# S5's matrices made in two parts: the GpSimd chain, and TensorE's share some FFN steps later

## The chip, the cores and the metric

The kernel runs on one core of a Trainium2 chip. The metric is the device time of one execution in microseconds; a kernel's time is the median of its runs. A profile of one execution gives, for each engine, every instruction with its start and duration, and what released it.

## The reference

Two layers of a decoder trunk on 256 tokens of 1024 features, in float32. Each layer is

```
x = x + 1/2 FFN_1(norm(x))                 # SwiGLU, 2816 hidden
h = norm(x)
x = x + (sum_b sigmoid(gate_b) * y_b) w_out    # b: mLSTM, S5, GLA, RWKV-7, each on 512 columns of h w_in
x = x + CrossAttention(norm(x), norm(mem))
x = x + 1/2 FFN_2(norm(x))
```

The change concerns the branch S5: 32 groups of 16 channels with 64 complex states each, run as a scan over the tokens.

```
bar  = exp(lam * step)                          # complex, one for each state
bb   = ((bar - 1) / lam) * (b_re + i b_im)      # [group, state, channel]
s_t  = bar * s_(t-1) + bb u_t
y_t  = Re(c s_t) + d u_t
z    = gelu(y);  y_b = (z glu_w1) * sigmoid(z glu_w2)
```

## The kernel before

**FFN.** `ffn` (line 377) opens a layer with 22 up steps, `f` = 0 to 21. A step takes a chunk of weights, two halves of 128 x 1024, each loaded by SP's queue (`chunk`, line 227), copied rounded by ScalarE (`whi`, line 242) and split by VectorE (`wlo`, line 243); then 48 TensorE products of 128 x 128 weights with 256 columns (three for each block: lines 257 to 259) and the activation on VectorE and ScalarE. The 8 down steps, `d` = 0 to 7, have 66 products each, and each ends in `x` plus the result (line 410).

**S5's matrices.** They hang on parameters alone, so they are made during the first FFN. `s5_ahead(at)` is called after each step, with `at` = f in the up steps and 22 + d in the down steps, and `S5_AT` says for each layer after which steps `s5_prep` and the four calls of `s5_mats` (line 1101), one for each feature tile, are traced. A call of `s5_mats` does the following:

- three loads from ScalarE's queue: `s5bc` (C) and the last block of `Bp` (B), lines 1111 and 1113
- on GpSimd a chain of complex products over 128 x 128 elements, B and C times powers of the state's factor: 48 operations (lines 1119 to 1135), then a memset of `In` (line 1144)
- on TensorE 8 transposes of `Bp` into the bank `wps` (line 1151), in two halves that ScalarE copies to `W` (line 1152), and 16 products of 64 columns into the bank `gps` (line 1157), which need the first 36 operations of the chain; the transposes need all 48
- ScalarE copies `gps` to `Gs` (line 1160), VectorE adds the skip term in four operations (line 1162), and six DMAs on ScalarE's queue put pieces of `Gs` into `In` (lines 1167 and 1170)

`s5` (line 1175) runs in the mix and takes `W`, `In` and `Cp` of tile after tile in `s5_tile`.

**The order of the work.** The program is traced as one list, and a planner makes each engine's queue from it with its own costs: among the instructions whose inputs are ready by these costs an engine takes the one traced first. `issue_after` adds an order, `high_priority` moves the weights' split to the front, and SP's queue keeps the traced order. On the chip each engine works its queue off in order and waits on semaphores. Tiles in SBUF get their places from the planner by how long they live; `Bp` has 128 x 1280 elements, `W` 128 x 1024. PSUM tiles of one tag share their banks: `wps` is in that of `br="y"`, `gps` in that of `br="s"`, one bank each.

The mix that follows (`mix`, line 601) norms `x` (its squares are summed on GpSimd, line 293, its low parts made there too, line 338) and takes five chunks of columns before the norm is there; then `rwkv` is traced, and the other branches in turns by the letters of `ORDER`.

Of the kernel before, what the change touches and what calls it, by code (L numbers as in the profile page):

```python
# [14 lines left out]
ALU = mybir.AluOpType  # L15
# [7 lines left out]
# of each layer: columns taken before the norm, when the memory is split, where S5's matrices are made, and the  # L23
# order in which the branches of the mix go ahead
LAZY = 5, 5
MEM_AT = 0, 0
S5_AT = (2, 7, 12, 15, 19), (3, 10, 16, 22, 26)
ORDER = ("SSDSSSDSSSGSDSSGSDSGDGDGDGDGDGDDGDGDGMDGMDGMMDMDMMDMDDDDDD",
         "SSSSSSSSSSSSDSDGDGDGDMGDMGDMGDMGDMGDMGDMGDMGDGDGDDDDDDDDDD")
POS = 0, 1, 3, 2, 4                  # where the steps of a block have their rows  # L30
# [23 lines left out]
class Arena:  # L54
    """Small tiles in rotation, cut from one tile."""
# [19 lines left out]
class K:  # L75
# [20 lines left out]
    def px(self, shape, n="px", br=None):  # L96
        """A PSUM bank of the branch at work."""
        br = br or self.br
        return self.ps.tile(shape, F32, tag="px" + br, name=self.nm(n), bufs=self.PX[br])

    def pd(self, n):
        """A PSUM bank for the large products."""
        return self.ps.tile([P, 2, T], F32, tag=self.pdt[0], name=self.nm(n), bufs=self.pdt[1])
# [13 lines left out]
    # ------------------------------------------------------------ set-up  # L117
# [28 lines left out]
    def consts(self):  # L146
# [9 lines left out]
        # an early use of the scalar engine's tables, so that they are there when the data is  # L156
# [5 lines left out]
        # columns for reductions over partitions  # L162
# [4 lines left out]
        # per-head-of-64 selectors (columns)  # L167
# [8 lines left out]
        # takes the mean over a head off  # L176
# [3 lines left out]
        # reset pattern for scans over chunks of 64  # L180
# [3 lines left out]
        # causal masks of a chunk of 64 of the delta rule: rows s (twice), columns t (twice): [r a] in an even  # L184
        # chunk, [a r] in an odd one, with s <= t for r and s < t for a
# [7 lines left out]
        # level masks for GLA: 1 where s in first and t in second half of the same block of 2m  # L193
        self.lvl = {}
        for mm in (16, 8, 4, 2, 1):
# [5 lines left out]
            # s >= 2mm*n  # L201
            nc.gpsimd.affine_select(out=f, in_=f, pattern=[[-2 * mm, nb], [0, 2 * mm]],
                                    compare_op=ALU.is_ge, fill=0.0, base=0, channel_multiplier=1)
            # s < 2mm*n + mm
# [3 lines left out]
        # rows to be spread over partitions: the parts of eight rows from 0 and from 32, and who takes which  # L208
# [11 lines left out]
    # ------------------------------------------------------------ helpers  # L220
# [6 lines left out]
    def chunk(self, dram):  # L227
        """A chunk of 16 blocks of weights, each half loaded and split on its first use: f(block) -> (hi, lo)."""
# [25 lines left out]
    def mm3(self, ps, w, x, first, last):  # L254
        """ps += w.T x in three passes of split operands."""
        nc = self.nc
        nc.tensor.matmul(ps, w[0], x[0], start=first, stop=False)  # L257
        nc.tensor.matmul(ps, w[0], x[1], start=False, stop=False)  # L258
        nc.tensor.matmul(ps, w[1], x[0], start=False, stop=last)  # L259

    def newton(self, x, n, parts=P):
        """1/sqrt(x) for x [parts, n], x > 0."""
# [12 lines left out]
    def bcast_rows(self, stat, groups, out_ps):  # L275
        """stat [128 tok, groups] for one token tile -> out_ps[m, tok] = stat[tok, m // (128 // groups)]."""
# [6 lines left out]
    def rstd_tok(self, x, last=False):  # L283
        """x [128, 8, 256] -> rsqrt(mean(x^2) + eps) [128 tok, tok tile]."""
# [19 lines left out]
    def rstd_row(self, x):  # L304
        """x [128, 8, 256] -> [128, 256] with rsqrt(mean(x^2) + eps) of each token on all partitions."""
        rs = self.sp.tile([P, T], F32, tag="rs", name=self.nm("rs"), bufs=1)
        self.rows(self.rstd_tok(x), rs)
        return rs
# [7 lines left out]
    def gained(self, x, gname):  # L316
        """x times the gain of its norm, split: hi, lo [128, 8, 256]; the rstd is left to the products' readers."""
# [10 lines left out]
    def norm(self, x, gname, rs=None):  # L328
        """RMS norm, split: returns hi, lo tiles [128, 8, 256]."""
# [11 lines left out]
    def prod(self, blk, ps, hi, lo, interleave=False):  # L341
        """ps[:, s, :] = two blocks of outputs over the 8 tiles of hi + lo."""
# [33 lines left out]
    # ------------------------------------------------------------ FFN  # L376
# [37 lines left out]
    def s5_ahead(self, at):  # L414
        """What S5 makes of its parameters alone, on the way."""
        for i, a in enumerate(S5_AT[self.l]):
            if a == at:
                self.s5_mats(i - 1) if i else self.s5_prep()

    # ------------------------------------------------------------ cross attention  # L420
# [8 lines left out]
    def mem_stats(self):  # L429
        """The rstd of the memory's tokens, as a column and as a row."""  # L430
# [12 lines left out]
    def mem_kv(self):  # L443
        """Keys [d, m] and values [m, d] of the memory."""
# [29 lines left out]
    def xattn(self):  # L474
# [20 lines left out]
        rq = self.tp.tile([P, 4], F32, tag="rq", name=self.nm("rq"))        # rstd / 16, and minus it  # L495
# [15 lines left out]
    def softmax(self, h, qs, rq, kT):  # L511
        """Weights of a head, [t, m]."""
# [20 lines left out]
    def head(self, h, e, v):  # L533
        """The output of a head, split."""
# [17 lines left out]
    def proj_k(self, wname, c, hi, lo, acc):  # L552
        """acc += the product over input tiles 2c, 2c + 1 (hi, lo [128, 2, T]); the last one adds to x."""
# [12 lines left out]
    # ------------------------------------------------------------ mixers  # L566
# [9 lines left out]
    def spill(self, t):  # L576
        """Puts a tile away in DRAM; the returned function brings it back."""
# [10 lines left out]
    def wtiles(self, c):  # L588
# [4 lines left out]
        if c < LAZY[self.l]:                            # not yet normed  # L593
# [44 lines left out]
    def dense(self, branches):  # L638
        """The products that wait for nothing else: the gates, and the memory's keys and values."""
# [23 lines left out]
    # ---- C: gated linear attention  # L663
    def gla(self):
# [21 lines left out]
        # log decays (times 16)  # L686
# [19 lines left out]
        # scores, transposed: the blocks of a token tile with itself and of the first with the second; the keys of  # L706
        # two heads are on top of each other, so the queries go in block-diagonally
        A = self.ot([P, 2, 2, 2, P], n="gA")       # [s, pair, tile, par, t]
        Ao = self.ot([P, 2, 2, P], n="gAo")        # [s, pair, par, t]
# [4 lines left out]
        Q = self.ot([P, 2, 4, 2, 64], n="gQ")      # twice [channel, pair and tile, par, t of a second half]  # L714
# [14 lines left out]
        for lv, m in enumerate((128, 64, 32, 16, 8, 4, 2, 1)):  # L729
# [39 lines left out]
            else:  # L769
                # only the second half of each block of 2m has columns to take  # L770
# [5 lines left out]
        # output, token-major  # L776
# [25 lines left out]
        # gate: o * silu(g), twice the value, without the gain  # L802
# [16 lines left out]
    def split_y(self, y, scale=None):  # L819
# [3 lines left out]
        if len(y.shape) == 4:                                        # step by step of blocks of four  # L823
# [5 lines left out]
        elif scale is not None and not isinstance(scale, float):     # a column for each tile  # L829
# [13 lines left out]
    # ---- A: mLSTM  # L843
    def mlstm(self):
# [14 lines left out]
        uc = th                                                # twice silu  # L859
# [8 lines left out]
        v = self.ot([P, 2, 4, P + 1], n="av")                   # with a column of ones, for the sums of weights  # L868
# [15 lines left out]
        # gates: rows 0..3 of R: M (then em at 64.., g at 32..)  # L884
# [30 lines left out]
        num = self.ot([P, 2, W], n="anum")                      # token-major  # L915
        s = sp.tile([P, 16], F32, tag="ast", name=self.nm("asts"))       # den (tt, h), mean square (tt, h)
# [59 lines left out]
        self.tap(f"ml_{l}", out)              # twice the value, without the gain  # L976
# [3 lines left out]
    # ---- B: S5  # L980
    def exp_acc(self, x, n):
        """exp(x) and exp(x) - 1 for x [128, n]."""
# [22 lines left out]
    def s5_prep(self):  # L1005
# [47 lines left out]
        # bar - 1, coef  # L1053
# [18 lines left out]
        # Four steps at a time: with L the state's factor of a step and s[k] the state's share of the steps before  # L1072
        # the block k, times L,
        #   s[k + 1] = L^4 s[k] + sum_q L^(4 - q) B u[4 k + q]
        #   y[4 k + p] = Re(C L^p s[k]) + sum_(q <= p) Re(C L^(p - q) B) u[4 k + q] + D u[4 k + p]
# [7 lines left out]
        # rotations by the steps of 1, 2, ... 64 blocks  # L1083
# [17 lines left out]
    def s5_mats(self, i):  # L1101
        """The matrices of a feature tile (four pairs of groups): input [(q, c), state], state to output
        [state, (p, c)], within a block [(q, c), (p, c)]."""
# [5 lines left out]
        Bp = self.ot([P, 4, 2, 5, 32], n="s5Bp")                     # B times powers 4, 3, 1, 2, 0  # L1109
# [16 lines left out]
        cv = lambda p: (Cp[:, :, 0, p, :], Cp[:, :, 1, p, :])        # of the real and imaginary part of s  # L1126
# [16 lines left out]
        with self.tc.issue_after(last.ins):  # L1143
            nc.gpsimd.memset(In, 0.0)
        W = self.ot([P, 4, 2, P], n="s5W")
# [7 lines left out]
        # Re(C L^m B): rows of L^2 B (m = 2, 3) and of B (m = 0, 1)  # L1153
# [21 lines left out]
    def s5(self):  # L1175
# [3 lines left out]
        for i in range(2):  # L1179
            ps = self.wtiles(15 + i)  # L1180
            up = self.ot([P, 2, 4, 64], n="bup")                # step by step of the blocks
# [3 lines left out]
        self.ys[1] = y, 0.5                   # twice the value  # L1185
        us = self.ot([P, 4, 4, 64], n="us")                     # [(q, c), tile, pair, block]
# [5 lines left out]
        for i in range(4):  # L1192
            yield from self.s5_tile(i, us[:, i], y)

    def s5_tile(self, i, us, y):
        """One feature tile: four pairs of groups."""
# [11 lines left out]
        # v = conj(E) w  # L1208
# [39 lines left out]
    # ---- D: RWKV-7  # L1248
    def rwkv(self):
# [6 lines left out]
        hv = sp.tile([P, 8], F32, tag="hv", name=self.nm("hv"))         # w0 / 2, a0 / 2  # L1256
        TS(hv[:, 0:4], self.vec("w0", 0, 4), 0.5, None, ALU.mult)
        TS(hv[:, 4:8], self.vec("a0", 0, 4), 0.5, None, ALU.mult)
        ka = sp.tile([P, 8], F32, tag="ka", name=self.nm("ka"))         # k_a / 2, 1 - k_a / 2
# [14 lines left out]
        # decay, in-context rate  # L1274
# [25 lines left out]
        # normalised keys  # L1300
# [431 lines left out]
```

## Time and profile before

| | |
|---|---|
| runs of the kernel | 1878.28, 1883.78 and 1884.1 us; median 1883.78 |
| span of the profiled execution, first to last instruction | 1876.7 us |
| the runs, above that span | 1.6 to 7.4 us, the median 7.1 |
| TensorE busy in the span | 1795.8 us (96%) |
| VectorE, ScalarE, GpSimd busy | 1303.0, 913.3, 494.7 us |
| mean granted TensorE clock | 0.978 of 2.4 GHz |

The profiled execution's own time is not listed apart from its span; what lies around a span is seen from the runs. Engines are called PE (TensorE), PEld (its weight loads), DVE (VectorE), ACT (ScalarE), POOL (GpSimd) and SP. In a group's line `out<-in` gives tiles by the program's names. The granted clock is a share of 2.4 GHz.

### The profile page before, as it was taken

Reading aid. Unit: us, or ns where it says so; the run is one execution under the profiler, and the core shown is the slowest. Engines: PE = TensorE matmul, PEld = TensorE weight load, DVE = VectorE, ACT = ScalarE, POOL = GpSimd, SP = SyncE. Lnnn points to the kernel's source line nnn. Section 1 sums busy time; section 2 is a strip of 40 time slices with the busy share of each in tenths; the row PEclk is TensorE's granted clock in tenths of the full one; section 3 lists DMA queues with packets and bytes.
Section 4 is the critical chain, followed back from the end, with each engine's and each line's share of the span. In section 5 each row is a group of like instructions: output and inputs, shape, how many; then the busy total and the mean of one; then the engine's idle time right before and its main releaser. Section 6 shows DMA issues by size and latency. Waiting matters only on the chain. (4 is left out here: it accounts for less than half of the span.)

```text
span 1876.7 us, 37100 instructions
## 1 busy us (share of the span) xinstructions
PE 1795.8 (96%) x14884; PEld 1758.4 (94%) x14884; DVE 1303.0 (69%) x2197; ACT 913.3 (49%) x1434; POOL 494.7 (26%) x733
## 2 busy tenths in 40 slices
PE   7899999999999999999999889999999999999997
PEld 7788999999999999999999888999999999999997
DVE  8766575987566776766597555779775767766653
ACT  4444355455554454544445334555554554545442
POOL 6688321131111130100153675212121003110001
PEclk9999999989999999999999989999999999999998
DMA  6555555446446754565656545644653576546553
GB/s 193 174 149 157 159 178 177 148 131 200 152 147 199 252 178 133 170 184 185 184 161 207 153 139 159 192 146 132 211 153 119 197 240 225 156 131 186 184 184 102
DMA packets 131852, 320.34 MB, mean 171 GB/s; under 512 B 45792, under 2 KB 50912, under 8 KB 131168
## 3 DMA queue, kind: packets, MB, share of 16 engines
q1 hardware_dynamic: 83664, 290.31, 49.1%
q10 hardware_dynamic: 48016, 27.67, 5.2%
q8 instruction: 116, 1.90, 0.4%
q14 instruction: 56, 0.46, 0.1%
HBM read 300.11 MB, written 16.52 MB: 169 GB/s over the span
## 5 line engine op out<-in xcount | busy, mean ns | idle before, releaser
L243 DVE TENSOR_TENSOR wlo<-wraw,whi 128x1024 fp32r<-128x1024 f32 x524 | 670.8, 1281 | 372.0 <-ACT whi L242 361.1
L242 ACT CAST whi<-wraw 128x1024 fp32r<-128x1024 f32 x524 | 546.7, 1046 | 655.5 <-issue 152.9
L259 PE MATMUL gu<-xhi,wlo 128*128 128x256 f32 x1344 | 383.7, 285 | 2.9 <-DVE wlo L243 2.9
L258 PE MATMUL gu<-xlo,whi 128*128 128x256 f32 x1344 | 385.5, 287 | 0.0
L257 PE MATMUL gu<-xhi,whi 128*128 128x256 f32 x1344 | 384.1, 286 | 0.0
L259 PEld LDWEIGHTS gu<-xhi,wlo 128*128 128x128 f32 x1344 | 261.0, 194 | 3.5 <-DVE wlo L243 3.5
L258 PEld LDWEIGHTS gu<-xlo,whi 128*128 128x128 f32 x1344 | 260.9, 194 | 0.6
L257 PEld LDWEIGHTS gu<-xhi,whi 128*128 128x128 f32 x1344 | 260.3, 194 | 0.5
L293 POOL TENSOR_TENSOR arena<-arena 128x256 f32<-128x256 f32 x69 | 72.2, 1046 | 578.9 <-ACT arena L291 576.3
L259 PE MATMUL dn<-ahi,wlo 128*128 128x256 f32 x704 | 200.9, 286 | 0.0
L258 PE MATMUL dn<-alo,whi 128*128 128x256 f32 x704 | 200.7, 286 | 0.0
L257 PE MATMUL dn<-ahi,whi 128*128 128x256 f32 x704 | 200.3, 285 | 0.0
L257 PE MATMUL gps<-hhi,whi 128*128 128x256 f32 x512 | 151.3, 296 | 3.5 <-ACT gst L1517 2.7
L258 PE MATMUL gps<-hlo,whi 128*128 128x256 f32 x512 | 149.6, 292 | 0.0
L259 PE MATMUL gps<-hhi,wlo 128*128 128x256 f32 x512 | 148.9, 291 | 0.0
L259 PEld LDWEIGHTS dn<-ahi,wlo 128*128 128x128 f32 x704 | 136.3, 194 | 0.2
L258 PEld LDWEIGHTS dn<-alo,whi 128*128 128x128 f32 x704 | 136.3, 194 | 0.2
L257 PEld LDWEIGHTS dn<-ahi,whi 128*128 128x128 f32 x704 | 136.1, 194 | 0.2
L257 PE MATMUL zin<-hhi,whi 128*128 128x256 f32 x384 | 111.3, 290 | 1.1 <-ACT gst L1517 1.1
L259 PE MATMUL zin<-hhi,wlo 128*128 128x256 f32 x384 | 109.9, 286 | 0.0
L258 PE MATMUL zin<-hlo,whi 128*128 128x256 f32 x384 | 109.6, 285 | 0.0
L257 PEld LDWEIGHTS gps<-hhi,whi 128*128 128x128 f32 x512 | 100.6, 197 | 6.7 <-ACT gst L1517 4.2
(528 smaller groups left out, 4381.7 us busy)
## 6 DMA issues: line engine op xcount, KB each, us to landing
wraw<-in_gu_dram SPq DMA_DIRECT2D x176, 512.0 KB, 4.0
wraw<-in_dn_dram SPq DMA_DIRECT2D x88, 512.0 KB, 4.2
wraw<-in_win_dram SPq DMA_DIRECT2D x68, 512.0 KB, 4.2
wraw<-in_gates_dram SPq DMA_DIRECT2D x64, 512.0 KB, 4.1
gd<-gst ACTq DMA_DIRECT2D x32, 256.0 KB, 2.1
wraw<-in_wk_dram SPq DMA_DIRECT2D x16, 512.0 KB, 3.7
wraw<-in_wv_dram SPq DMA_DIRECT2D x16, 512.0 KB, 3.6
gld<-gd SPq DMA_DIRECT2D x32, 256.0 KB, 3.9
```

The lines of the kernel that those rows point to most:

```text
L242: nc.scalar.copy(hi, raw)
L243: nc.vector.tensor_tensor(lo, raw, hi.bitcast(F32), ALU.subtract)
L257: nc.tensor.matmul(ps, w[0], x[0], start=first, stop=False)
L258: nc.tensor.matmul(ps, w[0], x[1], start=False, stop=False)
L259: nc.tensor.matmul(ps, w[1], x[0], start=False, stop=last)
L293: nc.gpsimd.tensor_tensor(acc, acc, sq, ALU.add)
```

## The change

`s5_mats` becomes a generator with a `yield` between GpSimd's chain and TensorE's share. `s5_ahead` runs it up to the `yield` at the old steps (`S5_AT`, unchanged); what follows, TensorE's transposes and products, ScalarE's copies, VectorE's additions and the six DMAs into `In`, is traced at the steps of the new `S5_PE`, by `s5_finish`. Step 30 of layer 0 does not occur in `ffn`; `s5` finishes a tile that is still open before it uses it.

```
+S5_PE = (18, 24, 27, 30), (16, 22, 26, 29)
...
     def s5_ahead(self, at):
         for i, a in enumerate(S5_AT[self.l]):
             if a == at:
-                self.s5_mats(i - 1) if i else self.s5_prep()
+                if i:
+                    self.s5_late[i - 1] = self.s5_mats(i - 1)
+                    next(self.s5_late[i - 1])
+                else:
+                    self.s5_late = {}
+                    self.s5_prep()
+        for i, a in enumerate(S5_PE[self.l]):
+            if a == at:
+                self.s5_finish(i)
+
+    def s5_finish(self, i):
+        if i in self.s5_late:
+            for _ in self.s5_late.pop(i):
+                pass
...
         In = self.ot([P, 4, P], n="s5In")
         with self.tc.issue_after(last.ins):
             nc.gpsimd.memset(In, 0.0)
+        yield
         W = self.ot([P, 4, 2, P], n="s5W")
...
         for i in range(4):
+            self.s5_finish(i)
             yield from self.s5_tile(i, us[:, i], y)
```

The rest of the diff takes comments out.

## Rows read from the trace of the kernel before

**Rows 1.** The page: TensorE's line, and its busy tenths in 40 slices.
```profile
PE 1795.8 (96%) x14884; PEld 1758.4 (94%) x14884; DVE 1303.0 (69%) x2197; ACT 913.3 (49%) x1434; POOL 494.7 (26%) x733
...
PE   7899999999999999999999889999999999999997
```

**Rows 2.** Waits of TensorE, longest first: us in total, times, longest.
```profile
PE gps L1157 <- POOL s5Bp L1123: 38.0, 8, 7.4
```

**Rows 3.** Timeline of TensorE behind the first stall: start, us, what.
```profile
94.20 0.48 PE L1157 MATMUL gps<-s5Cp,s5Bp 128*64 128x64 f32 x2 [7.37 <-POOL s5Bp L1123]
...
98.68 0.38 PE L258 MATMUL gu<-xlo,whi 128*128 128x256 f32 x1
98.90 0.28 PE L259 MATMUL gu<-xhi,wlo 128*128 128x256 f32 x1
99.02 0.28 PE L257 MATMUL gu<-xhi,whi 128*128 128x256 f32 x1
```

**Rows 4.** Stretches: length, busy (count) of PE, PEld, DVE, ACT, POOL, clock, DMA, GB/s.
```profile
199.00:248.00 49.00, 49.00 (x412) 49.00 (x411) 27.64 (x29) 23.49 (x31) 7.12 (x6) 1.00 0.59 179
86.55:99.02 12.47, 5.10 (x31) 4.44 (x29) 3.87 (x4) 3.06 (x7) 12.47 (x32) 0.73 0.35 108
127.87:136.50 8.63, 4.30 (x28) 3.73 (x27) 2.46 (x7) 1.70 (x3) 8.63 (x22) 0.80 0.38 101
154.76:163.80 9.04, 4.76 (x29) 4.10 (x28) 2.97 (x3) 1.12 (x3) 9.04 (x22) 0.62 0.38 125
188.87:197.90 9.03, 5.33 (x31) 4.67 (x30) 2.75 (x5) 1.29 (x2) 9.03 (x22) 0.62 0.41 119
1030.65:1041.00 10.35, 5.11 (x30) 4.44 (x29) 3.59 (x3) 1.81 (x3) 10.35 (x28) 0.67 0.16 55
1075.00:1085.40 10.40, 5.70 (x33) 5.04 (x32) 4.35 (x4) 1.81 (x3) 10.31 (x26) 0.67 0.17 50
1114.73:1122.90 8.17, 3.92 (x25) 3.31 (x24) 1.84 (x2) 0.46 (x2) 8.17 (x20) 0.79 0.35 123
1142.14:1150.25 8.11, 3.96 (x26) 3.34 (x24) 2.36 (x3) 2.13 (x4) 8.11 (x19) 0.79 0.39 133
```

**Rows 5.** Line 1157's matmuls: ns min/median/max, first and last start.
```profile
L1157 PE MATMUL gps<-s5Cp,s5Bp x128: 222/314/371, 94.2 to 1149.0; 128*64 128x64 f32 x128
```

**Rows 6.** FFN matmuls alone, from an FFN's start (last row: the down steps').
```profile
7.00:75.16 68.16, 60.81 (x455) 59.46 (x456) 6.04 (x9) 0.95 0.56 179
...
946.00:1015.69 69.69, 68.66 (x569) 68.42 (x570) 7.43 (x11) 1.00 0.62 187
946.00:1036.18 90.18, 83.91 (x694) 83.47 (x694) 9.47 (x14) 0.99 0.60 183
946.00:1059.40 113.40, 104.83 (x851) 103.68 (x852) 11.54 (x17) 0.97 0.58 173
...
1093.00:1096.97 3.97, 3.47 (x29) 3.59 (x30) 0.00 (x0) 1.00 0.64 185
```

**Rows 7.** Stretches of layer 1 in which the chain runs, columns as in rows 4.
```profile
1015.69:1030.65 14.96, 14.96 (x127) 14.96 (x126) 12.43 (x15) 7.35 (x12) 14.96 (x22) 1.00 0.65 196
1030.65:1036.18 5.53, 0.28 (x3) 0.08 (x2) 0.92 (x2) 0.40 (x1) 5.53 (x15) 0.82 0.30 103
...
1096.97:1114.73 17.76, 17.76 (x150) 17.76 (x149) 10.10 (x11) 8.76 (x12) 17.72 (x31) 1.00 0.70 200
```

**Rows 8.** A stretch of the first FFN, columns as in rows 4.
```profile
50.00:60.00 10.00, 7.85 (x65) 7.65 (x65) 10.00 (x8) 4.75 (x7) 8.69 (x6) 1.00 0.26 84
```

**Rows 9.** The skip term's additions (a group), and the DMA issues into `In`.
```profile
L1162 DVE SCALAR_TENSOR_TENSOR s5G<-consts,s5G 32x32 f32<-32x32 f32 x32 | 15.2, 530 | 24.0 <-ACT s5G L1160 23.9
...
L1167 ACTq DMA_DIRECT2D s5In<-s5G x32: 592/612/1070, 101.9 to 1156.2; - x32
```

**Rows 10.** S5's result in layer 0: last DMA issue, and its first reader.
```profile
L1245 ACTq DMA_DIRECT2D by<-zd x16: 309/442/721, 349.2 to 401.9; - x16
...
L827 ACT ACTIVATE yhi<-by x4: 654/662/663, 542.2 to 543.9; 128x256 fp32r<-128x256 f32 x4
```

## The prediction

> **What bounds the kernel now.** I read the page first: TensorE is busy for 1795.8 us of a span of 1876.7, so 80.9 us are idle, and the slices put the dips at the start and around the FFN that opens each layer [rows 1]. The list of waits, for TensorE alone, says whom it waits for: one line, the S5 products of line 1157, waits 38.0 us for GpSimd in eight waits, one for each feature tile, the longest 7.4 [rows 2]. No other entry of the list is above 8.0 in all, so the kernel is bound by TensorE's queue, and a microsecond of TensorE's is a microsecond of the span. The timeline of the first of the eight shows that a stall goes on after its end: the products start at 94.20 after 7.37 us of idling, and the FFN's matmuls behind them are 0.21 us apart until 98.9, and 0.12 from there [rows 3]. The table by stretches says why: in the stretches around the eight stalls the granted clock averages 0.62 to 0.80, against 1.00 in an undisturbed one [rows 4]. It fell to the lower of its two levels in the idling and rose some microseconds after work came back.
>
> **What the change removes.** The undisturbed stretch issues 412 matmuls in 49.00 us, 0.119 us each. The eight stretches are 76.20 us long together and hold 233 matmuls, worth 233 x 0.119 = 27.7 us; 48.5 us are lost, 38.0 of them waiting and 10.5 at the lower clock [rows 2, 4]. Two things may make it more. About three matmuls of each stretch had begun before it (they overlap), 24 x 0.119 = 2.9 us. And I priced the 128 small products of line 1157 like full matmuls, though they have 64 columns: the two or so that were issued before the clock fell took 222 ns, most took 314 [rows 5]; at half the price they add 128 x 0.06 = 7.7 us. The bounds are 48.5 and 59.1; I take 53.
>
> **Where the products go.** The program only marks places; each engine's order is the planner's, which takes the first instruction in traced order that is ready by its own timing. The rows bear this out: the products of layer 1's first tile are traced behind step 10, and 694 FFN matmuls = 14.46 steps of 48 stand ahead of them in TensorE's queue [rows 6]. The planner thought GpSimd done there; GpSimd was not. Traced later, the products stand behind all of the steps up to their new mark, unless TensorE idles in the plan. An up step is worth 48 x 0.119 = 5.7 us, a down step 66 x 0.119 = 7.85. So the question is whether GpSimd's chain is done at the new marks, and that has to be asked with a slower chain. While DVE splits weights and activations (12.43 us busy of 14.96) an operation of the chain takes 14.96 / 22 = 0.68 us; in the stall behind it, with DVE busy for 0.92 of 5.53, it takes 5.53 / 15 = 0.37; over the down steps it takes 17.76 / 31 = 0.57 [rows 7]. Today the stall itself speeds the chain up. Without it, 36 operations to the products and 48 to the transposes take 24 and 33 us in the up steps, 21 and 27 in the down steps. The Trainium skill ("GPSIMD Engine Reference", Key points) has a rule for this, that GpSimd shares its SBUF interfaces with VectorE and contends with VectorE's instructions of two SBUF inputs; the splits are of that kind, the trace agrees, and the rule speaks against the change, since every stall taken away lengthens the chains.
>
> Chain by chain [rows 6, 7]. Layer 0, tile 0: its chain starts after 455 matmuls, step 9.5, and the new place is behind step 18, 19.0: 9.5 x 5.7 = 54 us for 33. Tiles 1 and 2 are marked two and five down steps beyond the up steps and have more. Layer 1, tile 0: from 569 / 48 = 11.85 to 17.0 are 29.4 us; enough for the products, 3 us too few for the transposes, which come first in the program. Tile 1: from 851 / 48 = 17.73 to the end of the first down step, 4.27 x 5.7 + 7.85 = 32.2 us for 33: about 1. Tile 2: from 29 / 66 = 0.44 to 5.0 down steps, 35.8 us: done. Tile 3's chain stands behind tile 2's in GpSimd's queue, with memsets and sums some 105 operations of 0.57 to 0.61, 60 to 64 us, and from 0.44 to 8.0 are 59.3: 1 to 5 us late, I take 3. The sum is 3 + 1 + 3 = 7 us of waits; the bounds are nothing (the planner puts products ahead of transposes, or matmuls between) and 14. Idling this short did not cost the clock: TensorE is idle for 2.15 of the 10 us from 50 on, and the clock is 1.00 there [rows 8].
>
> **What moves with them.** No instruction is added. ACT's three copies and six DMA issues (0.6 us each) and DVE's four additions of the skip term (0.53 us each) move with the products [rows 9]. The DMA issues stand in ACT's queue ahead of weight copies, and what is queued behind them is the split of the next weights; 5 us of ACT in a step in which it is half idle, and 2 us of DVE, which idles 2.5 us in three steps' worth of 15, are hidden behind weights already split. If that cover were gone TensorE would wait for what does not fit into the idle time of a step, 5 - 2.9 us of ACT and 2.1 - 0.95 of DVE, 1 to 2 us a tile. I cost it at nothing. The loads of the next tile's parameters stay at their marks; SP's queue is not touched.
>
> Layer 0's tile 3 has mark 30, which the FFN never reaches (its last is 29), so it is made when S5 asks for it, in the mix. Its products are ready long before; the planner can put them in any gap. Below: nothing. Above: one wait of TensorE on the six late DMAs, priced by the longest wait with its clock, 7.4 + 2. S5 itself has room: its last result is issued at 401.9 and first read at 542.2 [rows 10]. I take 1 us.
>
> The sum is 53 - 7 - 1 = 45 us: a span of 1876.7 - 45 = 1831.7. The three runs stand 1.6 to 7.4 us above the profiled span, the median 7.1; I add 3.3 and forecast **1835 us**.
>
> **The rivals.**
> *Half of it comes back.* The longer chains matter more than I think: in layer 1 each tile waits at its new place as long as now, clock and all. For it: three of the four margins above are within 3 us of nothing. Against it: they are within 3 us, not 5. Layer 0's four stretches last 39.17 us and hold 119 matmuls, 14.2 us: 25 us, with a share of the upper bound 27, remain. 1884 - 26 = 1858. It decides from a rate of about 0.75 us an operation.
> *The products stay where they were.* TensorE idles somewhere in the plan while the products are ready, and the planner fills the gap with them, near the old places. For it: the planner's liking for the first ready instruction. Against it: TensorE's waits in the steady steps are next to none [rows 2]. Nothing gained: 1884.
> *Slower.* The B matrices with their powers (128 x 1280, 5 KB a partition) live longer. If the planner admits tiles 2 and 3 of a layer only when the FFN's hidden activations are free, both chains (96 operations, 64 us) start at the FFN's end, and the norm's last steps stand behind them in GpSimd's queue. Two column chunks of 5.7 us cover 11.4, the rest is idling: 2 x (64 - 11.4) = 105 against 53 gained, 1884 + 52 = 1936. It decides from 38 us late in each layer. Against it: what is put off, W with 4 KB, is nearly as large as what is kept, so space is no tighter by more than 1 KB a tile.
>
> **How the numbers follow.** Forecast 0.71, half 0.16, no change 0.08, slower 0.05. About 0.3%, 5.6 us, is what a measurement of this kernel can tell from no change; so faster 0.87, same 0.07 (no change, less a little), slower 0.06. The forecast's own range is 1878.3 - 59 = 1819 (all of the upper bound, on the lowest run) to 1884 - 48.5 + 14 + 2 = 1852. The two at the end leave out 0.13 together, the half case (1858) must be in: 1818 to 1860.
>
> **What would show it.** Right: the eight waits on GpSimd in line 1157's place gone from TensorE's list but for a few microseconds in layer 1; a granted clock of 1.00 over both opening FFNs; operations of the chain near 0.65 us, none at 0.37 in a row; the products of layer 0 at up step 19 and down steps 3 and 6. Wrong: waits of 4 us and more on the chain's last operations, above all at layer 1's tiles 0 and 3; norm sums late at the start of layer 1's mix; gaps at tile 3's input matrix in layer 0's mix; or idling in the mixes, whose order is planned anew, which no row here can price.

## The result: 1.6% faster, and the profile after

The changed kernel takes 1851.65 us, the median of five runs (1847.71 to 1860.55), against 1883.78 of the kernel before (five runs, 1878.15 to 1890.89): a ratio of 0.984, interval 0.982 to 0.987. The forecast was 1835 in a range of 1818 to 1860, so the median lies inside it, 16.65 us above the forecast. The profiled execution has a span of 1858.8 us. It is the slowest of its five (the other four spans are 1846.0 to 1850.6), while the profiled one of before, 1876.7, was among the fastest of its kernel. The two traces therefore differ by 17.9 us where the medians differ by 32.1. The slowest execution also has the lowest mean granted clock of the five, 0.979 against 0.983 to 0.985. Each of the five times lies about 1.7 us above its own span.

The page of the changed kernel, TensorE's line and two of its slices:

```profile
PE 1794.1 (97%) x14884; PEld 1757.8 (95%) x14884; DVE 1302.3 (70%) x2197; ACT 912.2 (49%) x1434; POOL 527.5 (28%) x733
...
PE   7989999989999999999999999999999999999997
PEclk9989999999999999999999999988989999999999
```

The work is the same as in [rows 1], by the count of instructions on each engine; GpSimd alone is busier, 527.5 us for the same 733 operations. TensorE's dips in layer 1's first FFN (slices 23 and 24 of before) are gone; slice 3 has one, in layer 0's FFN, and the clock has dips in slices 27, 28 and 30, in layer 1's mix.

TensorE's waits in the changed kernel up to the mix of layer 1, longest first (us in total, times, longest):

```profile
PE ss L297 <- POOL arena L294: 8.7, 1, 8.7
...
PE gps L258 <- ACT gst L1534: 3.2, 2, 2.7
...
PE wps L1167 <- POOL s5Bp L1138: 0.3, 1, 0.3
```

All eight waits of [rows 2], 38.0 us, are gone; 0.3 us stand at the transposes of layer 1's first tile. A wait of 8.7 us has appeared that the list of before did not have: the product of the memory's statistics (`mem_stats`, traced at up step 10 of layer 0), whose seven sums are made on GpSimd.

The table by stretches, first the changed kernel, then the one before: FFN and mix of layer 0, FFN and mix of layer 1. Columns as in [rows 4].

```profile
8.20:230.60 222.40, 206.56 (x1671) 204.33 (x1672) 165.54 (x265) 103.36 (x158) 159.44 (x264) 0.96 0.59 178
230.60:671.40 440.80, 429.89 (x3662) 415.75 (x3660) 327.95 (x564) 227.25 (x365) 84.37 (x74) 0.99 0.56 176
932.80:1131.30 198.50, 198.08 (x1666) 196.78 (x1665) 149.53 (x232) 94.04 (x136) 152.21 (x241) 1.00 0.62 187
1131.30:1583.60 452.30, 442.73 (x3662) 429.49 (x3660) 317.39 (x563) 226.85 (x365) 80.99 (x75) 0.96 0.55 172
```

```profile
8.00:248.70 240.70, 215.03 (x1696) 211.48 (x1697) 163.81 (x269) 105.57 (x161) 153.15 (x264) 0.94 0.55 166
248.70:685.70 437.00, 432.19 (x3637) 418.94 (x3636) 324.52 (x560) 225.09 (x363) 80.33 (x74) 0.98 0.56 178
946.50:1173.00 226.50, 208.15 (x1690) 205.60 (x1689) 152.92 (x235) 95.84 (x139) 135.29 (x241) 0.95 0.55 164
1173.00:1603.10 430.10, 426.35 (x3638) 413.66 (x3636) 318.53 (x558) 226.18 (x362) 75.15 (x74) 1.00 0.56 180
```

This table shows where the two profiled executions differ. The FFNs gave back 18.3 and 28.0 us, 46.3 together. The mixes took 3.8 and 22.2, which is 26.0. What lies between and behind took 2.4, so that 28.4 us of the gain are lost again. In the medians it is less: if the FFNs give 46.3 us there too, which no run lists by stage, 46.3 - 32.1 = 14.2 us are lost. About half of the 28.4 would then be the chance of these two executions. Only some 24 of a mix's 3662 matmuls are new (tile 3's). In layer 1 the mean clock fell from 1.00 to 0.96.

Where the 22.2 us went is read in the mix itself. TensorE's waits there in the changed kernel, the largest two of the list; before, no entry was above 1.1:

```profile
PE zin L258 <- ACT VU L1399: 4.1, 1, 4.1
PE px L1440 <- DMA Tw<-dW: 2.4, 1, 2.4
```

TensorE's timeline of the changed kernel, ahead of the first of these waits and behind the second (start, us, what):

```profile
1287.13 0.28 PE L259 MATMUL gps<-hlo,whi 128*128 128x256 f32 x1
1287.25 0.28 PE L260 MATMUL gps<-hhi,wlo 128*128 128x256 f32 x1
...
1354.48 1.65 PE L1440 MATMUL px<-Tw,L 32*32 32x32 f32 x32 [2.42 <-DMA Tw<-dW]
...
1356.65 0.41 PE L260 MATMUL zin<-hhi,wlo 128*128 128x256 f32 x1
1356.87 0.41 PE L258 MATMUL zin<-hhi,whi 128*128 128x256 f32 x1
```

Full products start 0.12 us apart ahead of it and 0.21 to 0.22 apart behind it. The stretches around three places, with the clock in the third column from the end:

```profile
1219.00:1232.00 13.00, 12.23 (x63) 11.92 (x64) 12.02 (x31) 4.68 (x8) 0.00 (x0) 0.61 0.31 83
1290.40:1300.40 10.00, 5.89 (x28) 5.81 (x28) 6.30 (x16) 6.94 (x13) 3.03 (x4) 0.66 0.57 173
1351.90:1368.60 16.70, 14.28 (x136) 13.32 (x135) 4.99 (x8) 5.34 (x14) 3.30 (x3) 0.59 0.39 125
```

These are 39.7 us at a mean clock of 0.61 to 0.62. So the mix lost less by waiting than by what followed. In the trace's clock records the mix of layer 1 has 37.5 us at the lower level, 3.4 before; each such microsecond does about half the work, so 34.1 more are worth 17. Gaps above 0.7 us from the start of one product to the start of the next, less the usual 0.12, hold 10.6, 3.5 before: 7.1. Tile 3's products add about 1.9 of work. These make 26 where 22.2 are to be explained; the parts overlap and are rough.

### The profile page after: what moved, and what is told of

The parts are those of the page before. It is cut to its first block, busy times and chain, and to the rows that moved or that the text cites. A ratio compares the mean times of both kernels' runs of the same rounds, so it can differ in the third digit from the quotient of the medians.

```text
span 1858.8 us, 37108 instructions
## 1 busy us (share of the span) xinstructions
PE 1794.1 (97%) x14884; PEld 1757.8 (95%) x14884; DVE 1302.3 (70%) x2197; ACT 912.2 (49%) x1434; POOL 527.5 (28%) x733
## 4 chain that ended last, share of the span: by engine, by line
PE 51%; DVE 4%; issue 3%; DMA 2%; POOL 2%; ACT 1%; ACTq 0%; POOLq 0%; DVEq 0%
PE gu L259 6%; PE gu L258 6%; PE gu L260 6%; PE dn L258 3%; PE dn L259 3%; PE dn L260 3%; PE acc L576 2%; DVE wlo L244 1%; PE gps L259 1%; PE zin L258 1%; PE gps L258 1%; PE zin L260 1%; PE zin L259 1%; PE gps L260 1%; PE gu L354 1%
```

## The experiments

Each run is compared with the kernel before on the same chip, whose medians were 1880.79 to 1882.66. Every version computes all of the reference. The theories named A, B and C in the expectations concern the mix of layer 1: that the planner's new order of it costs the time (A), that TensorE's early arrival does (B), or that the profiled clock was bad luck (C). How alike two orders are is the share of TensorE's instructions of that mix that match in sequence: the changed kernel's is 0.87 alike to that of before.

**One layer at a time.** Layer 1 alone deferred, layer 0 at the old places:

```
-S5_PE = (18, 24, 27, 30), (16, 22, 26, 29)
+S5_PE = (7, 12, 15, 19), (16, 22, 26, 29)
```

> Layer 0 makes its matrices as before, layer 1 as in the change. The profiles before and after differ by stage: layer 0's first FFN gave 18.3 us (240.7 to 222.4), its mix cost 3.7 (437.0 to 440.7), layer 1's first FFN gave 28.0 (226.5 to 198.5), its mix cost 22.3 (430.0 to 452.3). Theory A, the loss in a mix is the new order that the planner makes of it: layer 0's stages are those of before (240.7 and 437.0), layer 1's FFN is 198.5, and layer 1's mix, whose order is a third one here, neither that of before nor that of the change, lies anywhere from 430 to 455, not just at 452. Theory B, the loss comes because TensorE reaches the mix some 28 us sooner than the other engines and the transfers are ready for it, whatever the order: the mix of layer 1 is at 450 again. Theory C, the profiled run of the change was an unlucky one: 430 to 435. Span by A 1849 to 1874, by B 1870, by C 1850.

Layer 0 alone:

```
-S5_PE = (18, 24, 27, 30), (16, 22, 26, 29)
+S5_PE = (18, 24, 27, 30), (10, 16, 22, 26)
```

> Layer 0 as in the change, layer 1 as before. Layer 0's first FFN takes 222 us with one wait of about 9 us for GpSimd's sums of the memory's squares (line 297), its mix 441 in the change's order; layer 1's FFN has its four waits again (226) and its mix the order of before but for a thousandth of it. Theories A and C: layer 1's mix 430, span about 1862. Theory B, which ties the loss to the time that the FFN of the same layer gave back: 430 too, and layer 0's mix pays 4 us for 18. With the layer-1 kernel the gains add up to that of the change if the layers are independent.

Layer 1 alone took 1860.89 us, 0.989 (0.986 to 0.992); layer 0 alone 1868.11, 0.993 (0.990 to 0.996). The gains, 21.8 and 14.5 us, are 36.3 together, against 32.1 for both layers at once. With layer 1 alone the FFN of layer 1 took 198.5 us and its mix, in a third order, 447.6 us, which A and B both allow. With layer 0 alone the mix of layer 1 came out in its old order (0.999 alike) and took 429.8 at a clock of 1.00. The new wait at the statistics' product was there again, 10.2 us.

**The statistics' sums earlier.** `mem_stats` at up step 5, ahead of all chains:

```
-            if f == 10 and self.mcol is None:
+            if f == 5 and self.mcol is None:
```

> The change, and the memory's statistics (squares on ScalarE, sums on GpSimd, one TensorE product) are traced after up step 5 in place of step 10, ahead of GpSimd's chain for tile 0 and not behind it. The orders of both mixes are those of the change. If the 8.7 us wait of line 297 is the old stall at its next reader, GpSimd's queue being late against the plan, it goes, and the clock's fall with it: layer 0's first FFN from 222.4 to about 211 us, span of a comparable run down by 11, time about 1841. Rival: the wait is for the loads of the memory, or the chain behind the sums is now late and TensorE waits at its transposes: FFN stays at 220 or more, time 1850.

1852.91 us, 0.985 (0.982 to 0.988); nothing gained. The wait at the product only moved, to 66.71 with 6.4 us: at step 5 the sums stand behind `s5_prep`'s operations on GpSimd. The FFN took 221.0. The mix of layer 1, in exactly the order of the changed kernel, took 445.1 us.

**Tile 3 a down step earlier**, with the sums early:

```
+S5_PE = (18, 24, 27, 29), (16, 22, 26, 28)
```

> As the kernel with the early statistics, but the last tile's mark is 29 in layer 0 (in the FFN, not in the mix) and 28 in layer 1. With these the planner gives layer 1's mix the order of before to 99 parts in 100 (87 in the change). Layer 1's FFN may wait about 5 us and lose 2 at the lower clock at mark 28, because tile 3's chain ends near down step 7.6. Theory A: layer 1's mix at 430 to 434 us, as before, though TensorE reaches it some 45 us sooner; time about 1841 - 20 + 7 = 1828 if the early statistics gave their 11. Theory B: mix at 450, time 1848. Theory C: both kernels alike but for the 7 us.

1852.99 us, 0.984 (0.979 to 0.989). The mix of layer 1 came out 0.993 alike to the old order and took 436.4: 16 us less than in the changed kernel's profile, but 8.7 less than in the run with the sums early, which differs by the marks of tile 3 alone. The FFN of layer 1 gave 7.4 us back (205.9), 3.3 of them a wait for tile 3's chain at the earlier mark.

**Four that separate order, arrival and queue.** The statistics in down step 4 of layer 0 in place of up step 10:

```
+            if d == 4 and self.mcol is None:
+                self.mem_stats()
```

> The change, with the memory's statistics (seven sums on GpSimd, their squares on ScalarE) moved from layer 0's up step 10 to its down step 4, where GpSimd has no chain left. Theory (the wait of 8.7 us at the statistics' product is GpSimd being behind with tile 0's chain): no wait over 1 us on GpSimd is left in layer 0's FFN, which goes from 222.4 us (and 221.0 with the sums at up step 5) to about 210, the 8.7 and the stretch at half clock behind it. Rival (the sums themselves cost, wherever they lie): a wait of some 6 to 9 us moves into the down steps, and the FFN stays at 220 to 222. The mix of layer 1 is again in a new order, so by theory A it stays at 445 to 452. Time 1838 to 1845 by the theory, 1852 by the rival.

1849.47 us, 0.984 (0.982 to 0.986). The theory fell: the wait at the product went, and one of 8.8 us stood at 154.37, at the first down product. ScalarE's timeline of that run there:

```profile
147.72 0.41 ACT L394 ACTIVATE arena<-zz 128x256 f32<-128x256 f32 x1
161.32 0.35 ACTq L441 DMA_DIRECT2D mraw<-in_memT_dram  x1
161.79 1.05 ACT L243 CAST whi<-wraw 128x1024 fp32r<-128x1024 f32 x1 [13.65 <-POOL s5Bp L1135]
```

The planner had put the loads of the memory (line 441) early into ScalarE's queue; the second waited there until 161.32, behind operations of tile 3's chain, and the copies of the weights behind it waited as well. The FFN took 223.1. The mix of layer 1 came out in yet another order, 0.95 alike to the changed kernel's and 0.88 to that of before, and took 436.8. So an order need not be the old one to be good.

Tile 3 of layer 1 alone, all else at the old places:

```
+S5_PE = (7, 12, 15, 19), (10, 16, 22, 29)
```

> The kernel before, but for one thing: the products of tile 3 of layer 1 come behind down step 7 in place of up step 26's place. The waits of tiles 0 to 2 of layer 1 stay, so TensorE reaches the mix at about its old time; the order of layer 1's mix on TensorE comes out as in the run with layer 1 alone changed. Theory A (the new order costs the mix its time): mix of layer 1 at 443 to 450 us, against 430.0 before, and the gain of tile 3's wait (about 5 us) is more than eaten: 1885 to 1895. Theory B (it costs because TensorE arrives early, before GpSimd and the DMA queues are ready): mix at 430 to 433, time about 1878.

1883.26 us, 1.001 (0.999 to 1.003). FFN and mix of layer 1, columns as above:

```profile
942.60:1162.90 220.30, 204.42 (x1666) 202.43 (x1665) 150.21 (x236) 94.39 (x136) 140.62 (x241) 0.96 0.56 169
1162.90:1614.90 452.00, 442.32 (x3661) 428.76 (x3660) 319.24 (x564) 226.13 (x366) 82.93 (x74) 0.96 0.55 172
```

The three waits of the FFN are still there, TensorE reaches the mix at 1162.9 (before: 1173.0), and the mix takes 452.0, in the very order of the run with layer 1 alone. So a mix can be that slow without early arrival, which speaks for A against B. The size is not settled by it: the profiled execution took 1892.33 us, the longest of ten (1880.38 to 1892.33). The median is 1.3 us above that of the kernel before, whose FFN of layer 1 took 6.2 us more. If the FFN gave that much in the median execution too, the rest of the kernel lost 7.5 us there, not 22.

The old order with early arrival, sums in down step 4:

```
+S5_AT = (2, 7, 12, 15, 19), (3, 9, 15, 20, 24)
+S5_PE = (18, 24, 27, 29), (16, 22, 26, 28)
```

> The change with the statistics in down step 4, and the marks of tile 3 a down step earlier in both layers (layer 1's chains begin one or two up steps earlier, so that they are done by then); the order of layer 1's mix on TensorE comes out as in the kernel before, to the last instruction. Theory A (order): mix of layer 1 at 429 to 433 us although TensorE reaches it some 30 us earlier. Theory B (early arrival): 440 or more. FFNs about 210 and 199. Time by A 1820 to 1830, by B 1832 to 1842.

1855.67 us, 0.987 (0.985 to 0.990). The mix, in the old order to the last instruction but reached 26 us earlier, took 434.7: 17.6 less than in the changed kernel, 4.6 more than before. The FFNs gave that away, 227.0 and 208.4. In layer 0 ScalarE's squares waited 18.1 us for GpSimd; in layer 1 a VectorE instruction whose like takes 0.67 us in the median (line 326, in the changed kernel's first FFN) took 10.53.

Layer 0's products right behind their chains, all else as in that run:

```
+S5_PE = (13, 19, 23, 26), (16, 22, 26, 28)
```

> As the run before it, but layer 0's products at marks 13, 19, 23 and 26, right behind the end of each chain, in place of 18, 24, 27 and 29. If the slack of several steps is needed, waits on GpSimd of 1 to 5 us come back in layer 0's FFN (212 to 220 us); if a chain of 25 to 35 us is all that has to be covered, none comes back (208 to 211). The order of layer 0's mix is a third one, 0.90 alike to the old: by theory A it costs 3 to 6 us against 437.0. Time 1820 to 1832.

1856.32 us, 0.987 (0.984 to 0.989). Both expected FFN times were missed (225.2): 5.2 us of waiting for the chain came back at mark 13, and 6.1 for ScalarE at the first down product. The mix of layer 0 took 442.3, that of layer 1, in an order 0.996 alike to the old one, 439.8: nearly 10 us more than in the kernel before.

**The sums behind the chain.**

```
-            if f == 10 and self.mcol is None:
+            if f == 12 and self.mcol is None:
```

> The change with the memory's statistics two up steps later, at step 12, ahead of tile 1's chain and behind the end of tile 0's. In the changed kernel tile 0's chain left GpSimd at 100.67 us and the sums ended at 107.6; step 12 begins some 10 us later than step 10. Theory (the wait is GpSimd being behind with a chain when the sums are queued): no wait over 3 us at the statistics' product, ScalarE not held by the squares, layer 0's FFN 209 to 213 us against 222.4. Rival (whatever is queued on GpSimd or behind it in this FFN meets a chain somewhere): one wait of 6 us or more shows up elsewhere, FFN 219 to 224. The order of layer 1's mix on TensorE is 0.95 alike to the change's. Time 1838 to 1846 by the theory, about 1850 by the rival.

1850.30 us, 0.983 (0.980 to 0.986). The rival held: FFN 224.4, with one wait of 11.2 us from 111.87. The mix of layer 1 took 439.5. VectorE's timeline there, and the stretch of its long instruction:

```profile
110.87 12.12 DVE L244 TENSOR_TENSOR wlo<-wraw,whi 128x1024 fp32r<-128x1024 f32 x1 [7.73 <-ACT whi L243]
122.91 0.68 DVE L392 TENSOR_TENSOR zz<-gu,arena 128x512 f32<-128x512 f32 x1
```

```profile
110.87:122.99 12.12, 1.00 (x9) 0.79 (x7) 12.12 (x2) 3.54 (x6) 12.12 (x26) 0.66 0.00 1
```

The split of a half chunk, 1.23 us in the median, took 12.12. GpSimd was busy for all of these 12.12 us, with 26 operations back to back; the loads stood still (1 GB/s), as SP's queue waits for that split, and TensorE ran nine matmuls. The changed kernel has the same at its new wait; VectorE, ScalarE and GpSimd there:

```profile
94.25 7.07 DVE L244 TENSOR_TENSOR wlo<-wraw,whi 128x1024 fp32r<-128x1024 f32 x1 [3.44 <-ACT whi L243]
104.12 1.27 DVE L244 TENSOR_TENSOR wlo<-wraw,whi 128x1024 fp32r<-128x1024 f32 x1 [2.79 <-ACT whi L243]
```

```profile
101.93 0.42 ACT L292 ACTIVATE arena<-mraw 128x256 f32<-128x256 f32 x1 [7.72 <-POOL arena L294]
```

```profile
99.79 0.44 POOL L1139 TENSOR_TENSOR s5Bp<-s5Bp,bu 128x128 f32<-128x128 f32 x1
100.18 0.52 POOL L1159 MEMSET s5In<- 128x512 f32 x1
100.67 6.97 POOL L294 TENSOR_TENSOR arena<-arena 128x256 f32<-128x256 f32 x7
```

From 94.25 to 101.32 GpSimd works without a gap (the chain, a memset, the first sum), and VectorE's split does not end before that. The seven sums start when chain and memset are done, at 100.67, and end at 107.64; ScalarE, whose squares wait for their buffers, cannot copy the next weights until 103.

**Both together**, the sums at step 12 and the old order:

```
+S5_AT = (2, 7, 12, 15, 19), (3, 10, 16, 21, 25)
+S5_PE = (18, 24, 27, 29), (16, 22, 26, 28)
```

> The run before it with layer 1's tiles 2 and 3 begun an up step earlier and tile 3's products a down step earlier in both layers; layer 1's mix on TensorE comes out in the order of the kernel before, to the last instruction. Layer 1's FFN 199 to 203 us (tile 3's chain has an up step more than in the run whose mark was also 28 and which waited 3.6 us there). Theory A: layer 1's mix 430 to 437 us, as in the other two runs with the old order (434.7, 436.4). Together with a layer 0 FFN of 209 to 213: 1825 to 1838. Rival: tile 3's chain meets the down steps' copies as in the run with the old order, one more wait of some 7 us: 1840 to 1848.

1853.70 us, 0.985 (0.982 to 0.988). The mix took 437.0 in the old order; the FFN of layer 0 took 222.1 with another split of 12.13 us on VectorE, that of layer 1 204.4 with a wait of 2.7 for tile 3's chain. Both FFNs took longer than expected.

**The changed kernel once more**, one execution:

> The changed kernel itself, once more. If the mix of layer 1 takes 452.3 us because of its order alone, it takes 450 to 453 again, with 35 to 38 us at half clock. If a part of it is the clock's chance, it comes out as in the run with the same order and the sums earlier: 444 to 447 with 15 to 20 us at half clock, and a span of 1848 to 1852 against 1858.8.

1855.30 us, span 1853.6. Its FFN of layer 0 and mix of layer 1:

```profile
8.00:227.30 219.30, 205.93 (x1671) 204.01 (x1672) 165.99 (x265) 103.50 (x158) 162.38 (x264) 0.97 0.61 182
1129.00:1578.80 449.80, 439.63 (x3662) 426.64 (x3660) 316.99 (x563) 227.20 (x365) 80.63 (x74) 0.97 0.55 173
```

449.8 lies between the two expectations: TensorE waits at the same two places (4.3 and 2.5 us; 4.1 and 2.4 in the profiled one), and 30.7 us are at the lower clock where the profiled one had 37.5 and the run with the same order and the sums early had 17.1. So part of the 22 is chance (C).

The mixes of layer 1 side by side. In the changed kernel's order, besides 452.3 and 449.8, the run with the sums early and the one below with the sums on VectorE:

```profile
1133.50:1578.60 445.10, 434.46 (x3660) 421.63 (x3660) 316.04 (x564) 226.62 (x365) 83.66 (x75) 0.98 0.55 175
1127.60:1572.00 444.40, 434.77 (x3662) 421.64 (x3660) 317.04 (x563) 226.89 (x365) 82.14 (x75) 0.98 0.56 175
```

In the old order, or 0.99 alike to it, and reached nearly as early: tile 3 a down step earlier, the old order, layer 0's products right behind their chains, and both together:

```profile
1144.10:1580.50 436.40, 428.65 (x3637) 415.96 (x3636) 319.30 (x559) 225.84 (x362) 77.04 (x74) 0.99 0.57 178
1146.80:1581.50 434.70, 430.51 (x3637) 417.79 (x3636) 320.76 (x561) 227.30 (x364) 77.43 (x74) 0.98 0.58 180
1141.30:1581.10 439.80, 429.41 (x3637) 416.46 (x3635) 319.38 (x559) 225.79 (x363) 74.34 (x74) 0.99 0.56 177
1135.30:1572.30 437.00, 430.72 (x3637) 417.82 (x3636) 319.91 (x558) 227.14 (x362) 76.82 (x74) 0.98 0.56 177
```

The two groups do not overlap; their means are 447.9 and 437.0. Of the 11 us between them about 1.9 are tile 3's products, which the second group has in the FFN; the order is left with some 9. The two runs whose order is 0.95 alike to the changed kernel's, with tile 3's products in the mix, took 436.8 and 439.5. The two executions that reach the mix late in the old order took 430.1 (before) and 429.8 (layer 0 alone), some 7 us less than the early ones; both are among the fastest of their kernels.

**The sums on VectorE**, at step 10:

```
-                nc.gpsimd.tensor_tensor(acc, acc, sq, ALU.add)
+                (eng or nc.gpsimd).tensor_tensor(acc, acc, sq, ALU.add)
...
+        y = self.rstd_tok(self.mem_tiles(), eng=self.nc.vector)
```

> The change with the memory's seven sums on VectorE in place of GpSimd, at step 10 as in the change; TensorE's order is that of the change throughout. In the changed kernel VectorE's split of a weight (1.25 us elsewhere) took 7.07 us from 94.25 on, up to the end of tile 0's chain on GpSimd, and 12.12 us beside an unbroken row of GpSimd's operations in the run with the sums at step 12. Theory (the two engines shut each other out: while GpSimd's chain runs without a gap, VectorE's operation does not get on): taking the sums off GpSimd leaves a wait of 4 to 8 us on TensorE there, because VectorE's split or a sum is held up for over 3 us until the chain ends; layer 0's FFN 215 to 220 us. Rival (the wait is only the sums' place in GpSimd's queue): no wait over 2 us, FFN 209 to 213. Layer 1's mix as in the change, 445 to 452. Time 1846 to 1852 by the theory, 1840 to 1845 by the rival.

1851.77 us, 0.984 (0.981 to 0.987). The numbers of the theory came (a wait of 4.6 us, FFN 215.8, mix 444.4), but not by its mechanism:

```profile
PE ss L297 <- DVE arena L294: 4.6, 1, 4.6
```

No VectorE instruction of that stretch took more than 1.6 us. The product came late because the sums stand between splits on VectorE and the squares wait for the memory's loads. So of the changed kernel's 9 us about half went with GpSimd's part in it, the queue and the shut-out together. What each of the two costs alone stays open.

None of these versions beats the changed kernel by what can be measured: those that defer both layers lie at 1849.5 to 1856.3, their ratios at 0.983 to 0.987.

## Why the prediction was right, and what it mis-sized

**The gain of the removed waits** was taken as 53 us with bounds of 48.5 and 59.1, and it came out near 53. Layer 1's FFN gave 28.0. Layer 0's gave 18.3 beside a new loss of about 11 (the wait of 8.7, and half of the 4.8 us at the lower clock behind it, from 107.69 to 112.45), so 29. Of the 57 together, 3.8 us are only moved, as tile 3's products of both layers now lie in the mixes; about 54 remain. That the stalls' price is 38.0 plus the slow clock behind them, as read from [rows 3, 4], is borne out.

**The 7 us of new waits in layer 1** were 0.3. The mechanism was right and the price a little high. The stretch of tile 0's chain in the changed kernel, columns as above:

```profile
1001.97:1032.60 30.63, 30.21 (x251) 29.82 (x250) 24.08 (x28) 14.40 (x21) 30.63 (x49) 1.00 0.60 188
```

49 operations without a gap in 30.63 us are 0.63 each, where 0.68 was forecast from [rows 7] and 0.37 had been the rate inside a stall [rows 7]. The chains did lengthen: tile 0's is done 0.33 us after TensorE is ready for the transposes. Tile 1's and tile 3's were done some 4 and 3 us ahead, where about 1 and 3 us too late was forecast.

```profile
1032.15 0.97 PE L1167 MATMUL wps<-consts,s5Bp 128*128 128x128 f32 x4 [0.33 <-POOL s5Bp L1138]
```

**The places** were as forecast: layer 0's products at up step 19 and down steps 3 and 6 with tile 3 in the mix, layer 1's at 17.0 and at the ends of down steps 1, 5 and 8.

**The step that failed** is the part "What moves with them". It asked what moves with the products, and left out who else reads GpSimd. The statistics' sums were queued behind tile 0's chain before, too, and TensorE's stall for tile 0 covered them. With that stall gone they are what TensorE meets next: 8.7 us, and 10.0 in the second execution. What is late next was asked for the chains alone. The runs show that it is no matter of one step: at up step 5, 10 or 12 or in the down steps, on GpSimd or on VectorE, layer 0's FFN stayed at 215.8 to 227.0 us, and a wait of 4.6 us or more stood somewhere in it each time: at the statistics' product, at a weight's split, at the transposes or at the first down product.

**Contention** was costed in one direction. The text cites the Trainium skill for GpSimd's chains growing slower beside VectorE; VectorE's splits were not made slower by GpSimd in any term. Beside GpSimd's unbroken rows they were: 7.07, 10.53, 12.12 and 12.13 us for single instructions. The trace of the kernel before already had one, behind the first stall:

```profile
96.35 3.81 DVE L243 TENSOR_TENSOR wlo<-wraw,whi 128x1024 fp32r<-128x1024 f32 x1 [8.13 <-ACT whi L242]
```

The Trainium skill ("Trainium Architecture — The Big Picture", What this means for kernel authors) calls the pair of ports that the two engines share an exclusive lock and not a split of bandwidth, which fits a shut-out in either direction; these rows agree with it, and none of them shows the lock itself.

**The mixes** were costed at 1 us, tile 3's in layer 0, and they cost 26.0 in the profiled pair. The prediction named this as what would make it wrong ("idling in the mixes, whose order is planned anew, which no row here can price"), but gave it no term and no share of the range's upper end. The runs show that the planner's new order costs part of it: some 9 of layer 1's 22.2 us by the executions set side by side above, and tile 3's products 1.9. The rest is not split: part is the chance of the profiled execution (452.3, where the same order took 444.4 in another run), and part may be early arrival, as all four executions of the old order reached early (434.7 to 439.8) took longer than the two reached late (430.1, 429.8). In the changed kernel's order the first wait has this cause on ScalarE:

```profile
1290.09 0.52 ACTq L1411 DMA_DIRECT2D Tp<-dA  x1
...
1293.36 0.58 ACT L1399 COPY VU<-px 64x512 f32<-64x512 f32 x1 [9.12 <-DMA Tp<-dA]
```

A load waits in ScalarE's queue for the store of its data, whose last part is issued at 1282.87 and lands at 1289.86, and holds the copies behind it for 9.1 us. ScalarE's queue in the kernel before:

```profile
1317.25 1.98 ACTq L1363 DMA_DIRECT2D dA<-L  x4
...
1322.49 0.52 ACTq L1394 DMA_DIRECT2D Tp<-dA  x1
...
1323.69 0.58 ACT L1382 COPY VU<-px 64x512 f32<-64x512 f32 x1
```

Two copies of weights and an activation stand there between the store and the load, the store lands at 1322.40, and the first `VU` copy starts without a wait. The wait stands in all four executions of the changed kernel's order (7.5 to 9.3 us) and in none of the old one. It is not the whole price of the order: the run with the sums in down step 4 has it too (7.8 us), and its mix took 436.8.

**The sum by spans**: a gain of 45 was forecast and the FFNs gave 46.3. That these agree is luck: 11 us of a stall that was not forecast stand against 7 of waits that did not come and 3.8 of work that only moved into the mixes. The mixes and the rest then took 28.4 in the profiled pair. In the times, the median gain is 32.1 us, 12.9 less than forecast. The other 3.8 of the 16.65 us lie in the step from span to time, for which 3.3 us were added where the median stands 7.1 above the profiled span. The range's upper end, 1852, takes tile 3's late DMAs at 2 us, though the text prices them at up to 7.4 + 2; with that it would have been 1859. Of the rivals, "half of it comes back" named 1858 and came near in number, by another way: nothing came back at the chains. "The products stay" and "slower" did not occur.

## What to carry to other kernels

When a stall is taken away, list everything else that is read from the late engine, and not only what is moved: the stall covered all of it, and the next reader takes over. Where a planner orders the queues, a moved instruction can reorder stages that the change does not touch; compare the order of those stages before and after, since here one order against another was worth some 9 us of 450, where the FFNs had given back 46. Compare several executions of each, as a single pair showed 22. Price a wait with the clock behind it: in the mix of the profiled execution 7 us of more idling came with 17 us lost to the lower clock.

## What the runs showed of the hardware

A VectorE instruction with two inputs can take ten times its usual length and more while GpSimd runs operations of two inputs without a gap. The splits of 128 x 1024 took 1.23 us in the median and 12.12 and 12.13 us beside 26 GpSimd operations in a row; a low part of 128 x 256 took 10.53. Beside the long ones the operations of GpSimd's chain took 0.39 to 0.46 us each, as in the first stall of the kernel before, where VectorE stood idle (0.39 to 0.45). When the split comes through, it is GpSimd's operation that takes 1.4 us. What decides between the two, these runs do not show: the changed kernel had it at up step 10 both times (7.07 and 7.47 us), the run with the sums on VectorE not at all.

TensorE's clock fell after short waits among small products in layer 1's mix of the changed kernel: a stretch of 16.70 us that opens with 2.4 us of waiting ahead of 32 x 32 products had a mean of 0.59, although TensorE was busy for 14.28 of it. The same mix before, whose longest waits are 1.1 and 0.8 us, was at the lower level for 3.4 us in all. A wait of 2.7 us ahead of full products, in layer 0's mix of the changed kernel (from 407.94), was not followed by the lower level.
